# A fifth buffer for the high parts and a fifth for the low parts of the streamed weights in an encoder trunk

## The chip, the cores and the metric

The kernel runs on one core of a Trainium2 chip. The metric is the device time of one execution in microseconds. Before the change the median of three runs is 1358.05 us (1356.56 to 1358.73).

## The reference, cut to what matters

Two layers work on 256 tokens of width 1024. Each layer is a half-step SwiGLU, a mixer of three branches (a state space branch S5, gated linear attention, grouped-query attention) with gates, and a second half-step SwiGLU. All of the large products have 256 rows on the one side and a weight matrix on the other.

```python
def swiglu_ffn(h, w_gate, w_up, w_down):
    return (jax.nn.silu(h @ w_gate) * (h @ w_up)) @ w_down

for i in range(DEPTH):                                   # DEPTH = 2
    x = x + 0.5 * swiglu_ffn(rms_norm(x, ffn1_norm[i]), ...)         # 1024 -> 2816 -> 1024
    h = rms_norm(x, mix_norm[i])
    (s5_u, gla_q, gla_k, gla_v, gla_g, gla_zf, gla_zb, at_q, at_k, at_v) = split(h @ w_in[i])
    y_s5, y_gla, y_attn = s5_branch(...), gla_branch(...), attn_branch(...)
    gates = sigmoid(h @ w_merge_gate[i] + b_merge_gate[i])           # one gate for each branch
    merged = sum over the branches of gate * (y @ w_branch)
    x = x + merged @ w_out[i]
    x = x + 0.5 * swiglu_ffn(rms_norm(x, ffn2_norm[i]), ...)
return rms_norm(x, final_norm)
```

## The kernel before

**Products in three parts.** Weights and activations are float32. Each is split into a high part (hi), which is the value rounded to the type that TensorE takes, and a low part (lo), which is the rest. `mm3` (L216) makes a product of 128 x 512 from three matmuls: hi by hi (L219), lo of the weight (L220), and lo of the activation (L221).

**Streaming the weights.** `load` (L193) brings weights in pieces of two k-steps of 128 rows by 512 columns, 512 KB. For each piece it takes a buffer of the pool `wraw` (5 buffers, tile `raw`), issues its DMA on SyncE's queue (L206), takes one buffer `hi` and one `lo` of the pool `whl` (4 buffers of each), casts raw into hi on ScalarE (L209), and subtracts hi from raw into lo on VectorE (L210). So a raw buffer is free once lo is made, and a pair of hi and lo is free once the last of its matmuls has run. There are 412 such pairs. A pair with 512 columns feeds 12 matmuls: two k-steps, two tiles of 128 tokens (t = 0 and 1), three parts. `stream` (L223) goes over the blocks of 512 columns of a matrix, and for each over the chunks of four k-steps; the hidden layer's blocks have four pairs each.

**Work beside the stream.** In the first and in the middle half-steps VectorE also makes the tables of the S5 branch (`s5_tables`, L529, lines L349 to L373), a layer ahead. In the mixers it carries the three branches' elementwise work and scans. `weave` (L94) interleaves these generators with the main stream. TensorE has small matmuls and transposes of these, and the transposes of the hidden activations (L298).

**What sets the order.** The kernel is written as a program of tiles; a scheduler then lays the instructions of each engine in one order, from a timeline of its own, in which a buffer that comes free earlier makes an instruction ready earlier. On the chip each engine follows its order. A buffer pool rotates, so that with four buffers the pair of piece n waits for the last matmul of piece n-4.

**Places named below.** L209 cast to hi; L210 subtraction to lo; L219 to L221 the three matmuls; L263 and L265 the norm's transposes and their scaling; L298 the hidden layer's transposes; L355 also the table `wa` of the mixer's gates, cast at L655; L980 and L1016 transposes of the gated linear attention.

Of the kernel before, what the change touches and what calls it, by code (L numbers as in the profile page):

```python
# [31 lines left out]
HD = 128  # L32
GH = 4
WPRIO = 0
WBUFS = (5, 4)
RA = 5
RG = 4
WSTEP = 2
# [87 lines left out]
class Enc:  # L126
    def __init__(self, tc, ctx, ins, out):
# [3 lines left out]
        self.const = pool("const", 1)  # L131
        self.wraw = pool("wraw", WBUFS[0])
        self.whl = pool("whl", WBUFS[1])
        self.hp = pool("hp", 1)
# [1044 lines left out]
```

## Time and profile before

| what | value |
|---|---|
| median of three runs | 1358.05 us |
| the profiled execution | 1357.79 us |
| its span, first to last instruction | 1356.0 us |
| TensorE busy in the span | 1310.3 us, 97% |
| VectorE busy | 1013.2 us, 75% |
| ScalarE busy | 703.5 us, 52% |
| granted TensorE clock, mean | 0.995 |

The profile's page gives busy time for each engine. Matmuls overlap in it: one of 512 columns has a duration of about 0.39 us, and the next starts 0.23 us after it, so time is counted from start to start. The view of waits gives, for the idle time of an engine, which instruction ended it. The view of stages gives busy time in windows of the span. The timeline lists instructions one after another, with the idle time before one in brackets.

### The profile page before, as it was taken

How to read it: one execution, taken by the hardware profiler on the slowest of the kernel's cores; microseconds unless marked ns; L12 is line 12 of the kernel's file. 1: busy time of each engine (PE TensorE's matmuls, PEld its weight loads, DVE VectorE, ACT ScalarE, POOL GpSimd, SP SyncE). 2: the span in 40 equal slices, each digit the busy share in tenths (PEclk: the TensorE clock that was granted, in tenths of full speed). 3: DMA queues.
4: the chain of work that ended last, by engine and by line, in shares of the span. 5: the costliest groups of instructions: out<-in, count | busy, mean ns of one | idle time of the engine just before them, and what ended most of it. 6: DMA issues, size and time to landing. Idle time of an engine off the chain costs nothing.

```text
span 1356.0 us, 19228 instructions
## 1 busy us (share of the span) xinstructions
PE 1310.3 (97%) x6792; PEld 1049.8 (77%) x6792; DVE 1013.2 (75%) x1794; ACT 703.5 (52%) x1106; POOL 76.9 (6%) x108
## 2 busy tenths in 40 slices
PE   7999999999999989999999999999999999999997
PEld 5877778877786778777877777888877867888886
DVE  6899985779995779997465765457899967655553
ACT  5545445547585445444354544355475854555542
POOL 1010220000100000210000000000001000000000
PEclk9999999999999989999999999999999999999999
DMA  7767666666452366666665655566665524555562
GB/s 230 189 214 232 219 226 189 202 223 218 163 182 78 117 161 208 196 208 215 195 196 180 196 164 189 187 177 217 226 210 156 174 68 148 191 177 181 183 209 77
DMA packets 201200, 249.87 MB, mean 184 GB/s; under 512 B 40856, under 2 KB 134600, under 8 KB 201104
## 3 DMA queue, kind: packets, MB, share of 16 engines
q1 hardware_dynamic: 200496, 247.59, 58.6%
q8 instruction: 53, 0.87, 0.3%
q10 hardware_dynamic: 608, 1.06, 0.2%
q14 instruction: 43, 0.35, 0.1%
HBM read 234.44 MB, written 13.11 MB: 183 GB/s over the span
## 4 chain that ended last, share of the span: by engine, by line
PE 58%; issue 18%; DVE 17%; DMA 4%; ACT 3%; POOL 1%; SPq 0%; POOLq 0%; ACTq 0%; DVEq 0%
PE mm L220 17%; PE mm L219 16%; PE mm L221 16%; DVE lo L210 5%; DVE t L349 2%; DMA raw<-in_ffn_w_gate 1%; DVE run L838 1%; DMA e<-scr 1%; PE as L1072 1%; PE ao L1094 1%; DVE run L837 1%; PE st L298 1%; ACT hi L209 1%; DMA raw<-in_ffn_w_up 1%; PE pt L263 1%
## 5 line engine op out<-in xcount | busy, mean ns | idle before, releaser
L210 DVE TENSOR_TENSOR lo<-raw,hi 128x1024 fp32r<-128x1024 f32 x412 | 499.0, 1218 | 178.8 <-ACT hi L209 174.1
L209 ACT CAST hi<-raw 128x1024 fp32r<-128x1024 f32 x412 | 427.8, 1043 | 309.0 <-PE mm L221 282.4
L220 PE MATMUL mm<-lo,hTh 128*128 128x512 f32 (+1 forms) x1120 | 444.0, 397 | 7.6 <-DVE lo L210 7.4
L219 PE MATMUL mm<-hi,hTh 128*128 128x512 f32 (+1 forms) x1120 | 436.4, 396 | 2.0 <-ACT hTh L267 2.0
L221 PE MATMUL mm<-hi,hTl 128*128 128x512 f32 (+1 forms) x1120 | 435.1, 392 | 0.0
L220 PEld LDWEIGHTS mm<-lo,hTh 128*128 128x128 f32 x1120 | 211.4, 189 | 53.0 <-DVE lo L210 11.9
L219 PEld LDWEIGHTS mm<-hi,hTh 128*128 128x128 f32 x1120 | 211.1, 189 | 44.4 <-ACT hTh L267 2.9
L221 PEld LDWEIGHTS mm<-hi,hTl 128*128 128x128 f32 x1120 | 210.7, 188 | 40.1 <-DVE hTl L268 0.2
L220 PE MATMUL mm<-lo,sThffn 128*128 128x512 f32 x352 | 138.3, 393 | 2.8 <-DVE lo L210 2.8
L221 PE MATMUL mm<-hi,sTlffn 128*128 128x512 f32 x352 | 137.4, 391 | 0.0
L219 PE MATMUL mm<-hi,sThffn 128*128 128x512 f32 x352 | 135.9, 393 | 0.0
L300 ACT CAST sThffn<-st 128x256 fp32r<-128x256 f32 x88 | 32.7, 372 | 129.9 <-PE st L298 129.5
L220 PEld LDWEIGHTS mm<-lo,sThffn 128*128 128x128 f32 x352 | 66.1, 188 | 17.7 <-DVE lo L210 3.7
L221 PEld LDWEIGHTS mm<-hi,sTlffn 128*128 128x128 f32 x352 | 66.1, 188 | 13.9
L219 PEld LDWEIGHTS mm<-hi,sThffn 128*128 128x128 f32 x352 | 66.0, 188 | 13.6
L301 DVE TENSOR_TENSOR sTlffn<-st,sThffn 128x256 fp32r<-128x256 f32 x88 | 37.1, 423 | 48.8 <-ACT sThffn L300 48.3
L294 ACT ACTIVATE t<-mm,rstd 128x256 f32<-128x256 f32 x88 | 41.5, 475 | 43.5 <-PE mm L221 41.1
L295 DVE SCALAR_TENSOR_TENSOR t<-mm,rstd,t 128x256 f32<-128x256 f32 x88 | 41.8, 482 | 13.6 <-ACT t L294 13.4
L298 PE MATMUL st<-ident,t 128*128 128x128 f32 x176 | 33.4, 272 | 0.5 <-DVE t L295 0.5
L298 PEld LDWEIGHTS st<-ident,t 128*128 128x128 f32 x176 | 24.3, 140 | 12.1 <-DVE t L295 0.9
L349 DVE TENSOR_TENSOR t<-e,S 128x512 f32<-128x512 f32 x32 | 20.2, 683 | 17.3 <-DMA e<-scr 17.2
L627 POOL COPY kx<-ks 128x128 f32<-128x128 f32 x32 | 18.9, 630 | 218.7 <-DVE ks L610 218.7
(357 smaller groups left out, 1440.0 us busy)
## 6 DMA issues: line engine op xcount, KB each, us to landing
raw<-in_ffn_w_gate SPq DMA_DIRECT2D x176, 256.0 KB, 3.8
raw<-in_ffn_w_up SPq DMA_DIRECT2D x176, 256.0 KB, 4.3
raw<-in_ffn_w_down SPq DMA_DIRECT2D x88, 512.0 KB, 4.6
raw<-in_w_in SPq DMA_DIRECT2D x48, 512.0 KB, 3.9
raw<-in_w_merge_gate SPq DMA_DIRECT2D x48, 512.0 KB, 4.6
raw<-in_w_out SPq DMA_DIRECT2D x16, 512.0 KB, 4.4
scr<-e SPq DMA_DIRECT2D x6, 768.0 KB, 5.5
e<-scr SPq DMA_DIRECT2D x6, 768.0 KB, 5.7
```

The source lines that it names most:

```text
L209: nc.scalar.copy(hi[:, :e - s, :width], raw[:, :e - s, :width])
L210: nc.vector.tensor_tensor(lo[:, :e - s, :width], raw[:, :e - s, :width], hi[:, :e - s, :width].bitcast(F32), op=ALU.subtract)
L219: nc.tensor.matmul(ps, act[0], w[0], start=first, stop=False)
L220: nc.tensor.matmul(ps, act[0], w[1], start=False, stop=False)
L221: nc.tensor.matmul(ps, act[1], w[0], start=False, stop=last)
L294: nc.scalar.activation(sg, ps[:, :256], AF.Silu, scale=rstd[:, t:t + 1])
L295: nc.vector.scalar_tensor_tensor(s, ps[:, 256:], rstd[:, t:t + 1], sg, op0=ALU.mult, op1=ALU.mult)
L298: nc.tensor.transpose(pt[:, j], s[:, j * P:(j + 1) * P], self.ident)
L300: nc.scalar.copy(h, pt)
L301: nc.vector.tensor_tensor(sl[:, 2 * b:2 * b + 2, t * P:(t + 1) * P], pt, h.bitcast(F32), op=ALU.subtract)
L349: self.nc.vector.tensor_tensor(out, a, b, op=ALU.mult)
L627: nc.gpsimd.tensor_copy(kx[:, :, s], ks.rearrange("p g j f -> p g (j f)")[:, :, (3 - s) * 16:(3 - s) * 16 + 64])
```

## The change

The constant that holds the number of buffers of `wraw` and of `whl` goes from (5, 4) to (5, 5). The pool `whl` holds hi and lo, so there is one more tile of each: 4 KB in each partition apiece, 8 KB together. The instructions are the same; the pair of piece n now waits for the last matmul of piece n-5. The scheduler makes a new order from it.

```diff
-WBUFS = (5, 4)
+WBUFS = (5, 5)
```

TensorE, at the end of the first half-step's hidden layer. mm290 and mm291 are the results of the last block for t = 0 and t = 1; hi_285, hi_288, hi_300 and hi_303 with lo_286 to lo_304 are its four pairs; hi_313 is the first pair of the next matrix. Before:

```order
L221 MATMUL mm291_1680<-hi_288_1675,hTl4_120 128x512
L219 MATMUL mm291_1680<-hi_300_1736,hTh4_119 128x512
L220 MATMUL mm291_1680<-lo_301_1737,hTh4_119 128x512
L221 MATMUL mm291_1680<-hi_300_1736,hTl4_120 128x512
L298 MATMUL st279_1624<-ident_79,t_279_1621 128x128 x2
L219 MATMUL mm291_1680<-hi_300_1736,hTh4_119 128x512
L220 MATMUL mm291_1680<-lo_301_1737,hTh4_119 128x512
L221 MATMUL mm291_1680<-hi_300_1736,hTl4_120 128x512
L219 MATMUL mm291_1680<-hi_303_1743,hTh4_119 128x512
L220 MATMUL mm290_1679<-lo_304_1744,hTh4_119 128x512
L221 MATMUL mm290_1679<-hi_303_1743,hTl4_120 128x512
L219 MATMUL mm290_1679<-hi_303_1743,hTh4_119 128x512
```

Now, at the same place:

```order
L221 MATMUL mm290_1679<-hi_300_1736,hTl4_120 128x512
L219 MATMUL mm290_1679<-hi_303_1743,hTh4_119 128x512
L220 MATMUL mm290_1679<-lo_304_1744,hTh4_119 128x512
L221 MATMUL mm290_1679<-hi_303_1743,hTl4_120 128x512
L219 MATMUL mm290_1679<-hi_303_1743,hTh4_119 128x512
L220 MATMUL mm290_1679<-lo_304_1744,hTh4_119 128x512
L221 MATMUL mm290_1679<-hi_303_1743,hTl4_120 128x512
L298 MATMUL st276_1615<-ident_79,t_276_1612 128x128 x2
L219 MATMUL mm291_1680<-hi_285_1668,hTh4_119 128x512
L220 MATMUL mm291_1680<-lo_286_1669,hTh4_119 128x512
L221 MATMUL mm291_1680<-hi_285_1668,hTl4_120 128x512
L219 MATMUL mm291_1680<-hi_285_1668,hTh4_119 128x512
```

Before, the fourth pair (lo_304) came after t = 1 had used the first three, for both tokens' tiles together; now t = 0 uses all of the four pairs, and then t = 1 begins with the first. The last matmuls of the first three pairs stand later in the block.

VectorE, at the same place: the subtraction lo_314, for the first pair of the next matrix, among table work. Before:

```order
L364 TENSOR_TENSOR U0_1062<-ef_416,eg_417 128x512
L365 TENSOR_TENSOR U1_1063<-ef_416,eg_417 128x512
L301 TENSOR_TENSOR sTlffn10_170<-st276_1615,sThffn10_169 128x2x128
L366 TENSOR_TENSOR U2_1064<-ef_416,eg_417 128x512
L368 TENSOR_TENSOR U3_1065<-ef_416,eg_417 128x512
L364 TENSOR_TENSOR T0_1118<-bb_297_1726,lpb_414 128x512
L365 TENSOR_TENSOR T1_1119<-bb_297_1726,lpb_414 128x512
L366 TENSOR_TENSOR T2_1120<-bb_297_1726,lpb_414 128x512
L368 TENSOR_TENSOR T3_1121<-bb_297_1726,lpb_414 128x512
L210 TENSOR_TENSOR lo_314_1798<-raw_312_1795,hi_313_1797 128x1024
L210 TENSOR_TENSOR lo_317_1804<-raw_315_1801,hi_316_1803 128x1024
```

Now:

```order
L210 TENSOR_TENSOR lo_304_1744<-raw_302_1740,hi_303_1743 128x1024
L301 TENSOR_TENSOR sTlffn10_170<-st255_1507,sThffn10_169 128x2x128
L364 TENSOR_TENSOR T0_1118<-bn_170_1067,coef_413 128x8x16
L295 SCALAR_TENSOR_TENSOR t_276_1612<-mm263_1529,rstd4_117,t_275_1611 128x256
L365 TENSOR_TENSOR T1_1119<-bn_171_1086,coef_413 128x8x16
L295 SCALAR_TENSOR_TENSOR t_279_1621<-mm264_1530,rstd4_117,t_278_1620 128x256
L366 TENSOR_TENSOR T2_1120<-bn_170_1067,coef_413 128x8x16
L368 TENSOR_TENSOR T3_1121<-bn_171_1086,coef_413 128x8x16
L210 TENSOR_TENSOR lo_314_1798<-raw_312_1795,hi_313_1797 128x1024
L369 TENSOR_TENSOR e_175_1123<-U0_1062,U1_1063 128x512
L373 TENSOR_TENSOR e_175_1123<-U2_1064,U3_1065 128x512
```

The subtraction stood behind eight rows of 512 columns and one of 256; these rows (U from ef and eg, T from bb and lpb) are behind it now, and shorter rows are ahead of it.

VectorE, in the first mixer: lo_657 among the work of the state space branch (t, run, e) and of the gated linear attention (la). Before:

```order
L210 TENSOR_TENSOR lo_654_3516<-raw_652_3513,hi_653_3515 128x1024
L349 TENSOR_TENSOR t_550_3055<-e_545_3038,run0_2591 128x512
L349 TENSOR_TENSOR t_552_3057<-e_545_3038,run0_2591 128x512
L355 TENSOR_TENSOR la0_3078<-t_561_3085,la0_3078 128x2x256
L355 TENSOR_TENSOR la0_3078<-t_562_3089,la0_3078 128x2x256
L355 TENSOR_TENSOR la0_3078<-t_565_3099,la0_3078 128x2x256
L355 TENSOR_TENSOR la0_3078<-t_566_3103,la0_3078 128x2x256
L210 TENSOR_TENSOR lo_657_3522<-raw_655_3519,hi_656_3521 128x1024
L352 TENSOR_TENSOR t_553_3058<-t_550_3055,t_552_3057 128x512
```

Now:

```order
L210 TENSOR_TENSOR lo_654_3516<-raw_652_3513,hi_653_3515 128x1024
L349 TENSOR_TENSOR t_550_3055<-e_545_3038,run0_2591 128x512
L349 TENSOR_TENSOR t_552_3057<-e_545_3038,run0_2591 128x512
L355 TENSOR_TENSOR t_551_3056<-t_550_3055,t_552_3057 128x512
L210 TENSOR_TENSOR lo_657_3522<-raw_655_3519,hi_656_3521 128x1024
L349 TENSOR_TENSOR t_550_3055<-e_545_3038,run0_2591 128x512
L349 TENSOR_TENSOR t_552_3057<-e_545_3038,run0_2591 128x512
L355 TENSOR_TENSOR la0_3078<-t_561_3085,la0_3078 128x2x256
L355 TENSOR_TENSOR la0_3078<-t_562_3089,la0_3078 128x2x256
L355 TENSOR_TENSOR la0_3078<-t_565_3099,la0_3078 128x2x256
L355 TENSOR_TENSOR la0_3078<-t_566_3103,la0_3078 128x2x256
L210 TENSOR_TENSOR lo_675_3632<-raw_673_3629,hi_674_3631 128x1024
```

The subtraction lo_657 has moved ahead of two multiplications of the scan's results and of the four rows of la.

## Rows read from the trace of the kernel before

**Rows 1.** Page, head: span; busy us (share of the span) xinstructions.
```profile
span 1356.0 us, 19228 instructions
PE 1310.3 (97%) x6792; PEld 1049.8 (77%) x6792; DVE 1013.2 (75%) x1794; ACT 703.5 (52%) x1106; POOL 76.9 (6%) x108
```
**Rows 2.** Waits, whole span: engine line <- releaser: us in total, times, longest.
```profile
ACT hi L209 <- PE mm L221: 282.4, 244, 5.2
...
PE mm L220 <- DVE lo L210: 10.2, 11, 2.0
```
**Rows 3.** Waits of TensorE in windows 130:260, 260:390, 520:650, 910:1040, 1040:1170.
```profile
PE mm L220 <- DVE lo L210: 2.8, 2, 2.0
...
PE mm L220 <- DVE lo L210: 2.9, 3, 1.7
...
PE mm L220 <- DVE lo L210: 2.8, 4, 1.2
...
PE mm L220 <- DVE lo L210: 1.0, 1, 1.0
...
PE mm L220 <- DVE lo L210: 0.7, 1, 0.7
```
**Rows 4.** Stages: window, busy us (x) of PE, PEld, DVE, ACT, POOL, PEclk, DMA, GB/s.
```profile
100.00:150.00 50.00, 47.96 (x313) 38.33 (x312) 50.00 (x105) 25.69 (x40) 6.86 (x9) 1.00 0.68 220
...
350.00:400.00 50.00, 48.27 (x296) 39.92 (x294) 49.79 (x89) 34.50 (x66) 5.93 (x3) 1.00 0.56 175
...
450.00:500.00 50.00, 44.03 (x195) 34.86 (x195) 36.56 (x78) 20.80 (x30) 1.65 (x2) 0.93 0.60 170
...
1200.00:1250.00 50.00, 50.00 (x229) 40.98 (x229) 29.06 (x36) 26.02 (x37) 0.00 (x0) 1.00 0.57 177
```
**Rows 5.** Timeline of TensorE at a wait: start, duration, instruction [idle before <-releaser].
```profile
151.80 0.39 PE L219 MATMUL mm<-hi,sThffn 128*128 128x512 f32 x1
152.96 0.50 PE L220 MATMUL mm<-lo,sThffn 128*128 128x512 f32 x1 [0.77 <-DVE lo L210]
```
**Rows 6.** Timelines of ScalarE, then VectorE, from 144.41 to 149.
```profile
144.41 1.05 ACT L209 CAST hi<-raw 128x1024 fp32r<-128x1024 f32 x1 [0.27 <-PE mm L221]
...
147.28 0.68 DVE L368 TENSOR_TENSOR T<-bb,lpb 128x512 f32<-128x512 f32 x1
147.88 2.35 DVE L210 TENSOR_TENSOR lo<-raw,hi 128x1024 fp32r<-128x1024 f32 x2
```
**Rows 7.** Timeline of TensorE: two transposes; an undisturbed run, both ends.
```profile
1200.53 0.38 PE L298 MATMUL st<-ident,t 128*128 128x128 f32 x2
1200.66 0.49 PE L220 MATMUL mm<-lo,hTh 128*128 128x512 f32 x1
1200.99 0.39 PE L221 MATMUL mm<-hi,hTl 128*128 128x512 f32 x1
...
1203.07 0.39 PE L221 MATMUL mm<-hi,hTl 128*128 128x512 f32 x1
...
1210.55 0.40 PE L221 MATMUL mm<-hi,hTl 128*128 128x512 f32 x1
```
**Rows 8.** Timelines from 487 to 492: ScalarE, VectorE, TensorE.
```profile
487.59 1.04 ACT L655 CAST wa<-wraw 96x1024 fp32r<-96x1024 f32 x1 [3.11 <-DMA raw<-in_ffn_w_gate]
...
488.67 1.21 DVE L355 TENSOR_TENSOR wa<-wraw,wa 32x1024 fp32r<-32x1024 f32 x1 [2.33 <-ACT wa L655]
...
491.25 1.11 PE L263 MATMUL pt<-ident,x 128*128 128x128 f32 x4 [4.27 <-DVE t L265]
```
**Rows 9.** Waits in 260:390, then 1040:1170; then timeline of VectorE.
```profile
PE goT L1016 <- DVE t L1013: 0.3, 1, 0.3
...
PE keT L980 <- ACT aqT L1060: 1.1, 1, 1.1
...
317.46 1.22 DVE L210 TENSOR_TENSOR lo<-raw,hi 128x1024 fp32r<-128x1024 f32 x1
318.59 1.29 DVE L349 TENSOR_TENSOR t<-e,run 128x512 f32<-128x512 f32 x2
```

## The prediction, made before the changed kernel ran

> **What bounds the kernel now.** I read the page's head first, then the waits of the whole span, then the waits and the stages window by window, and last the timelines at the waits. TensorE is busy for 1310.3 of 1356.0 us [rows 1]. That share alone does not say how near the end is, since matmuls overlap. The timeline does: one matmul of 512 columns starts 0.23 us after the one before, wherever nothing is late [rows 5, 7], and the stage from 1200 to 1250 runs like that with no idle time at all [rows 4]. So TensorE is the bound, and a change of buffers can win only what TensorE waits.
>
> The largest wait in the list, 282.4 us in which ScalarE's cast to hi waits for a matmul [rows 2], is the buffer limit itself: the cast is ready, raw has landed, and no pair is free. It costs nothing by itself, since ScalarE is busy for half of the span. What costs is the wait of TensorE for lo: 10.2 us in 11 waits, the longest 2.0 us [rows 2]. They lie in four groups [rows 3]: the tables of the first half-steps (2.8 us), the first mixer (2.9), the tables of the middle half-steps (2.8), the second mixer (1.0 and 0.7). In the others TensorE never waits for lo. Two stages show why: VectorE is busy for 50.00 of 50 us from 100 to 150 and for 49.79 from 350 to 400, against 29.06 in the stage without waits [rows 4]. The wait at 149.15, the longest, shows it closest: hi was ready at 145.46, and VectorE, with no gap, did table work until 147.88 before it came to the lo for which TensorE was waiting [rows 6].
>
> So in four stretches VectorE falls behind, eats the lead that the finished pairs give, and then TensorE waits, by less than 3 us in each. The question is how much lead one more pair gives there.
>
> **The change, part by part.**
>
> *What a wait costs.* At 152.96 a matmul starts 1.16 us after the one before, where 0.23 would do [rows 5]: 0.93 lost, and the row shows 0.77 idle. So each wait costs 0.16 more than its idle time, since the modelled end of a matmul covers it. The 11 waits cost 10.2 + 11 x 0.16 = 12.0 us. That is the most that can be won from them.
>
> *What one pair gives.* A pair feeds 12 matmuls, 12 x 0.227 = 2.7 us of TensorE's work. The 0.227 is the mean of the 33 steps from 1203.07 to 1210.55, an undisturbed run [rows 7]. If all of it became lead, once in each stretch that ends behind, the stretches would lose 3.1, 3.4, 3.4 and 2.0 us (idle time and 0.16 a wait) less up to 2.7 each: 0.4, 0.7, 0.7 and 0.0 are left, 1.8 together, and 10.2 is won. But the new order spends part of the lead. Before, the fourth pair of a hidden block was used at the block's end for both tiles at once; now t = 0 uses all four pairs before t = 1 begins, so that the first pairs are held longer. I counted, in both orders, the matmuls between the last use of a pair and the first lo of the piece that gets its buffer, at 0.227 us each: 7.2 us in the mean before and 10.0 now, but in the tightest tenth 5.2 before and 6.4 now. The mean grew by a whole pair, the tightest tenth by 1.2. With 1.2 in each of the four stretches the gain is 4.8 us. The bounds are 4.8 and 12.0. I take 9, nearer to the end that the mean stands for: at the very places of the waits VectorE's order helps too, since the eight table rows that stood ahead of lo_314, and the four rows of la that stood ahead of lo_657, now stand behind it.
>
> *What moves on TensorE.* Two transposes in the stream cost 0.13 us themselves, and the matmul behind them takes 0.33 instead of 0.23 to the next [rows 7]: 0.10 for each time that the stream of weight matmuls is broken. The order before has 253 such breaks and the new one 233. 20 x 0.10 = 2 us, bounds 0 and 2. I take 2.
>
> *What moves on VectorE.* The sum of its work is the same. One lo stands further ahead all along, so work of the branches stands later by a lo, 1.13 us from start to start [rows 9]. TensorE waits for branch work in a few places today: goT 0.3 and keT 1.1 in one mixer [rows 9], and such waits can grow. If each of some six places that wait at all grows by a third of a lo, 6 x 0.4 is 2.4 us; I take 2. The bounds are 0 and 6.8 (six times 1.13).
>
> *DMA.* A raw buffer comes free when its lo is made, so the loads run up to one piece further ahead. The bytes are the same and DMA is at 0.57 of its time where TensorE is full [rows 4]; this costs nothing, and if the cover were gone it would show as casts that wait for raw.
>
> *What stays.* At 491.25, ahead of the third half-step, TensorE stands for 4.27 us. The scaling of the norm stands behind the last update of x, that behind the subtraction for the table wa, that behind its cast, which waited 3.11 us for a load [rows 8]. [...] In the new order this chain is the same, with the same loads ahead of that of wa and one weight load more. [...]
>
> *The sum.* -9 for the waits, -2 for the breaks, +2 for branch work: -9. The profiled execution took 1357.79 us, its span 1356.0 us, 0.26 us under the median of the three runs. 1358.05 - 9 = 1349.
>
> **The rivals.**
>
> *The waits move on (no change).* VectorE is full in the stretches, and its work is not reduced. If a fuller lead only lets the scheduler put more table work ahead of the next lo, TensorE waits there instead. For it: in the new order 3.9 us of table rows stand between lo_314 and lo_317, where the two followed each other. Against it: the second lo is wanted later by a piece. Of the gain of 11 some 1 to 2 would be left: 1356 to 1357.
>
> *Branch work comes late (slower).* In each mixer four heads of the gated linear attention pass through VectorE, TensorE and back, with the transposes keT (L980) and goT (L1016), 16 places in both mixers. Where a lo put ahead delays the rows of a head by 1.13 us [rows 9] and nothing covers it, TensorE, which keeps its order, waits: 16 x 1.13 = 18 us, less 12 won, makes 1364. It decides from about 11 of 16 places: then the cost passes the 12.0. For it: lo_657 stands ahead of the four rows of la now, and every head starts from la. Against it: those places wait little today [rows 9], so most have room; and TensorE would need its stream of weights to be behind them in the order everywhere. The trace bears out the order that this needs: VectorE came to lo_314 only after all rows ahead of it, though hi was ready 2.4 us earlier [rows 6]. [...]
>
> [...]
>
> **How the numbers follow.** About 0.2%, 2.7 us, is what a measurement of this kernel can tell from no change: faster is under 1355.3, slower is over 1360.8. The forecast, with its bounds (from 1358.05 - 12.0 - 2 to 1358.05 - 4.8 + 2, so 1344 to 1355), gets 0.66; the stand that goes, 0.06; waits that move on, 0.17; branch work that comes late, 0.11. The range leaves out the stand that goes and the slower rival, 0.17 together, and takes in the waits that move on, with a little room: 1343 to 1358.5. Faster is 0.72, within 0.2% is 0.17, slower is 0.11.
>
> **What would show it.** In the profile after: TensorE's waits for lo fall from 10.2 us to about 2, with single ones left in the four stretches; the casts wait less for matmuls than 282.4 us; TensorE's busy time stays within some 3 us of 1310.3, and its idle time falls by about 9. The stand at about 490 is there again with a clock of about 0.93 in its stage. Waits for keT and goT together stay under 6 us. The prediction is wrong if the waits for lo stay over 6 us (the lead is spent by the order), or if they go and the span does not follow (then the idle time is at branch work, or at the stand).

## The result, and the profile after

The changed kernel takes 1345.63 us (median of four runs, 1344.8 to 1346.58), the kernel before 1357.93 (1356.56 to 1358.73). The ratio is 0.9908, with a 95% interval of 0.9894 to 0.9923: 12.3 us or 0.9% faster. The forecast was 1349.0 with a range of 1343.0 to 1358.5. The profiled execution took 1344.8 us.

The head of the page after, which answers [rows 1]:

```profile
span 1343.0 us, 19230 instructions
PE 1305.5 (97%) x6792; PEld 1053.9 (78%) x6792; DVE 1009.0 (75%) x1794; ACT 698.2 (52%) x1106; POOL 87.6 (7%) x108
```

The span is 13.0 us shorter. TensorE's idle time, span less busy, falls from 45.7 us to 37.5, by 8.2; its busy time falls by 4.8, with the same 6792 matmuls. So more than a third of the gain is not in any wait.

Waits of the whole span, after (engine, line, releaser: us in total, times, longest), which answers [rows 2]:

```profile
ACT hi L209 <- PE mm L221: 300.6, 251, 5.8
...
ACT hi L209 <- DMA raw<-in_ffn_w_up: 14.3, 13, 3.5
...
PE mm L220 <- DVE lo L210: 4.0, 2, 2.1
```

TensorE's waits for lo fell from 10.2 us in 11 places to 4.0 in two. The casts wait longer for matmuls than before, 300.6 against 282.4.

Where the time went is read best by stage. A stage begins here with the first weight matmul of 512 columns behind the norm's transposes. In some kernels four of the sixteen transposes of a norm stand behind that matmul, so that the length of a stage is good to about 0.8 us. Stages before, in the order of the program (two half-steps with a mixer between them, for each of two layers); window, busy us of PE, PEld, DVE, ACT, POOL, then PEclk, DMA, GB/s:

```profile
10.68:217.74 207.06, 202.42 (x1093) 162.20 (x1093) 184.71 (x441) 102.13 (x146) 29.15 (x40) 1.00 0.70 215
217.74:492.02 274.28, 261.99 (x1457) 208.46 (x1457) 219.70 (x346) 158.95 (x284) 10.07 (x11) 1.00 0.56 174
492.02:693.49 201.47, 196.97 (x925) 157.89 (x924) 161.03 (x383) 95.69 (x131) 16.27 (x25) 0.99 0.64 195
693.49:893.83 200.34, 199.61 (x1023) 158.84 (x1022) 124.18 (x166) 94.37 (x135) 9.29 (x15) 1.00 0.58 183
893.83:1161.42 267.59, 260.66 (x1459) 208.39 (x1458) 216.34 (x328) 157.74 (x283) 9.10 (x8) 1.00 0.56 175
1161.42:1356.00 194.58, 186.20 (x839) 152.37 (x837) 105.47 (x127) 91.68 (x128) 1.39 (x2) 0.98 0.52 165
```

The same stages after:

```profile
10.95:213.08 202.13, 201.62 (x1097) 162.74 (x1097) 183.44 (x442) 102.51 (x148) 31.21 (x40) 1.00 0.72 222
213.08:487.37 274.29, 263.03 (x1455) 210.14 (x1454) 219.83 (x346) 157.72 (x284) 12.90 (x10) 0.99 0.56 174
487.37:682.82 195.45, 194.84 (x926) 158.51 (x924) 159.54 (x383) 95.25 (x131) 20.95 (x25) 0.99 0.65 200
682.82:877.55 194.73, 194.22 (x1023) 158.26 (x1022) 123.85 (x166) 93.73 (x135) 9.11 (x15) 1.00 0.60 188
877.55:1148.66 271.11, 263.30 (x1459) 210.12 (x1458) 217.31 (x328) 156.98 (x283) 10.38 (x8) 0.99 0.55 173
1148.66:1343.00 194.34, 186.00 (x839) 152.53 (x837) 103.21 (x126) 89.06 (x127) 1.39 (x2) 0.99 0.52 163
```

The differences are -4.9, 0.0, -6.0, -5.6, +3.5 and -0.2 us, and +0.3 ahead of the first stage: -13.0, the whole of it. The two half-steps with waits for lo won 4.9 and 6.0, most of it idle time (4.64 us to 0.51, and 4.50 to 0.61). Of these 8.0 us of idle time 5.6 were waits for lo. Another 1.3 in the first stage were a wait for a load, ahead of the transposes cT (L560) at 73.69; it is gone too. The fourth stage won 5.6 although TensorE was idle there for only 0.73 us before; its busy time fell by 5.4. The mixers, the second and the fifth stage, won nothing, and the second of them lost. (Before, four transposes stand inside the first mixer; in the changed kernel none do, so with the same work in it that mixer lost some 0.8 us too.)

**The fourth stage.** There the S5 branch makes tables for the next mixer. For each of four blocks of a layer's tables TensorE runs 48 small matmuls into `kp`, 16 of 128x32 (L597) and 32 of 64x96 (L603). Three of the four blocks are made in this stage, one in the third. Timeline of TensorE in the stage, before (start, duration, instruction, count):

```profile
782.03 0.39 PE L219 MATMUL mm<-hi,hTh 128*128 128x512 f32 x1
782.35 0.35 PE L603 MATMUL kp<-cc,bb 64*32 64x96 f32 x2
782.63 0.50 PE L220 MATMUL mm<-lo,hTh 128*128 128x512 f32 x1
782.96 0.39 PE L221 MATMUL mm<-hi,hTl 128*128 128x512 f32 x1
```

And after:

```profile
788.69 0.39 PE L221 MATMUL mm<-hi,hTl 128*128 128x512 f32 x1
789.01 0.33 PE L597 MATMUL kp<-cq,bb 128*32 128x32 f32 x16
789.27 0.56 PE L603 MATMUL kp<-cc,bb 64*32 64x96 f32 x32
789.76 0.50 PE L219 MATMUL mm<-hi,hTh 128*128 128x512 f32 x1
790.10 0.39 PE L220 MATMUL mm<-lo,hTh 128*128 128x512 f32 x1
```

Before, two small matmuls between two large ones made 0.93 us from 782.03 to 782.96, where two undisturbed steps take 0.45: 0.48 lost. After, all 48 of a block stand in one place and make 1.41 us from 788.69 to 790.10: 0.96 lost. So the price is that of the place, about 0.46, and 0.01 for each small matmul in it. In the stage's timeline before they stand in 19 places, after in 6. Thirteen places fewer at 0.46 are 6.0 us; 5.6 were won. Added up over the whole stage, the steps with such matmuls in them and the steps right behind lose 10.5 us before and 4.5 after, against 0.227 a step. The scheduler's new order did this; no wait is in it.

**The mixers.** Waits of TensorE in the windows 260:390 and 1040:1170 of after, which answer [rows 9], with the wait for lo of 910:1040 between them:

```profile
PE goT L1016 <- ACT aqT L1060: 1.5, 1, 1.5
...
PE mm L220 <- DVE lo L210: 2.1, 1, 2.1
...
PE kv L995 <- ACT t L1080: 0.9, 1, 0.9
```

Each mixer has one wait for lo now (1.93 us and 2.1), and one of 1.5 us for goT. Counted in weight matmuls from the start of the mixer, the wait for lo stands at the 535th in the first mixer and at the 536th in the second. TensorE, before, in the first mixer, at the 391st and at the 535th:

```profile
323.74 0.50 PE L220 MATMUL mm<-lo,hTh 128*128 128x512 f32 x1 [1.67 <-DVE lo L210]
...
367.09 0.50 PE L220 MATMUL mm<-lo,hTh 128*128 128x512 f32 x1 [0.74 <-DVE lo L210]
```

So the place waited before too, 0.74 us, and 0.73 at the 536th matmul of the second mixer. The earlier waits (1.67 and 0.47 us in the first mixer, 1.04 in the second) are gone; the one that is left has grown. Timeline of VectorE ahead of it in the first mixer, after (several instructions of one kind are one row):

```profile
349.88 1.22 DVE L210 TENSOR_TENSOR lo<-raw,hi 128x1024 fp32r<-128x1024 f32 x1
351.01 1.21 DVE L837 TENSOR_TENSOR_SCAN run<-e,t 64x511 f32<-64x511 f32 x1
...
356.97 1.29 DVE L349 TENSOR_TENSOR t<-e,run 128x512 f32<-128x512 f32 x2
358.17 1.22 DVE L210 TENSOR_TENSOR lo<-raw,hi 128x1024 fp32r<-128x1024 f32 x1
```

VectorE works through 7.16 us of scans and other side rows, from 351.01 to 358.17, between two subtractions. Before, subtractions at 358.51 and 362.43 stood among the same kinds of rows, and the longest stretch between two from there on was 2.79 us. TensorE at the end of it, after:

```profile
357.19 0.33 PE L855 MATMUL yp<-mt,U 64*64 64x64 f32 x4
359.45 0.75 PE L220 MATMUL mm<-lo,hTh 128*128 128x512 f32 x1 [1.93 <-DVE lo L210]
...
360.42 0.63 PE L219 MATMUL mm<-hi,hTh 128*128 128x512 f32 x1
360.85 0.63 PE L220 MATMUL mm<-lo,hTh 128*128 128x512 f32 x1
```

Behind the wait the matmuls start 0.43 us apart, not 0.23. Three windows of 3.5 us, ahead of, in and behind this stretch:

```profile
356.00:359.50 3.50, 1.57 (x11) 0.96 (x9) 3.50 (x7) 3.49 (x7) 0.57 (x1) 1.00 0.00 0
359.50:363.00 3.50, 3.50 (x11) 2.82 (x12) 3.50 (x7) 0.82 (x2) 0.00 (x0) 0.51 0.51 158
363.00:366.50 3.50, 3.50 (x17) 2.86 (x17) 3.50 (x6) 2.37 (x5) 1.44 (x1) 1.00 0.70 219
```

The 1.57 us of TensorE's work in the first window are what the wait of 1.93 leaves of it: until the wait TensorE ran large matmuls, and four small ones last. Behind the wait the granted clock was 0.51 from 359.5 to 363.0, and 1.00 again in the window after that. By an estimate from these rows, 0.49 of the work of 3.5 us is lost at 0.51 of the clock, 1.7 us; the second mixer has such a fall too, 0.52 from 1025.0 to 1028.5, about 1 us behind its wait. So the wait of 1.93 us cost about 3.6 there, by this estimate.

**The stand ahead of the third half-step** is there again, in TensorE's timeline and in the stage from 450 to 500, which answer [rows 8] and [rows 4]:

```profile
486.61 1.12 PE L263 MATMUL pt<-ident,x 128*128 128x128 f32 x4 [4.19 <-DVE t L265]
...
450.00:500.00 50.00, 44.14 (x195) 34.98 (x194) 34.63 (x80) 20.57 (x30) 1.65 (x2) 0.93 0.59 156
```

### The profile page after: what moved, and what is told of

Same layout as the page of the kernel before. It is cut to its first block, busy times and chain, and to the rows that moved or that the text cites. A ratio compares the mean times of both kernels' runs of the same rounds, so it can differ in the third digit from the quotient of the medians.

```text
span 1343.0 us, 19230 instructions
## 1 busy us (share of the span) xinstructions
PE 1305.5 (97%) x6792; PEld 1053.9 (78%) x6792; DVE 1009.0 (75%) x1794; ACT 698.2 (52%) x1106; POOL 87.6 (7%) x108
## 4 chain that ended last, share of the span: by engine, by line
PE 67%; issue 16%; DVE 10%; ACT 3%; DMA 2%; SPq 0%; POOL 0%; POOLq 0%; ACTq 0%; DVEq 0%
PE mm L219 20%; PE mm L220 19%; PE mm L221 19%; DVE lo L210 3%; PE st L298 1%; DVE t L349 1%; ACT hi L209 1%; DMA raw<-in_ffn_w_up 1%; PE as L1072 1%; DVE run L838 1%; PE ao L1094 1%; PE S L820 1%; DVE run L837 1%; PE yp L858 1%; PE apt L1087 1%
## 5 line engine op out<-in xcount | busy, mean ns | idle before, releaser
L209 ACT CAST hi<-raw 128x1024 fp32r<-128x1024 f32 x412 | 427.7, 1043 | 330.9 <-PE mm L221 300.6
L617 POOL TENSOR_TENSOR e<-r,tcst 128x512 f32<-128x512 f32 x8 | 25.4, 3180 | 152.0 <-DVE r L349 82.4
L298 PEld LDWEIGHTS st<-ident,t 128*128 128x128 f32 x176 | 23.8, 140 | 10.2
```

The lines of the kernel that those rows point to most:

```text
L209: nc.scalar.copy(hi[:, :e - s, :width], raw[:, :e - s, :width])
L298: nc.tensor.transpose(pt[:, j], s[:, j * P:(j + 1) * P], self.ident)
L617: nc.gpsimd.tensor_tensor(ld["e"][:, SCR_R - SCR_E:].rearrange("p (g c) -> p g c", g=GQ), self.r4[:, gs].unsqueeze(2).to_broadcast((P, GQ, ...
```

## The experiments

My theory after the result had three parts: the fifth pair gives lead in the half-steps with tables, the new order groups the small matmuls, and the mixers give something back. The rivals: lo alone or hi alone does it; the loads do it; grouping is a by-product that costs nothing by itself. "Stage" below is the length of a stage, found as above.

**A fifth lo alone, a fifth hi alone, more raw buffers.** Three kernels with one size changed each:

```diff
-                lo = self.whl.tile([P, SUB, 512], F32R, name=self.nm("lo"), tag="lo")
+                lo = self.whl.tile([P, SUB, 512], F32R, name=self.nm("lo"), tag="lo", bufs=5)
```

> Five buffers for lo, four for hi. The order of every engine is that of the kernel before, row for row; only the rotation of the lo buffers differs. Theory 'lead' (TensorE stops waiting because finished pairs run further ahead): a lo needs its hi, and the fifth hi is missing, so nothing runs ahead: the time of before, 1358 us within 0.2%, waits of TensorE for lo about 10 us. Theory 'order' (the gain is the scheduler's new order and has little to do with waits): the same time too, since the order is the old one. A faster time by 3 us or more would say that the lo buffers alone were what bound.

Measured: 1358.2 us, ratio 1.0001 (0.999 to 1.0011). The order is that of before.

```diff
-                hi = self.whl.tile([P, SUB, 512], F32R, name=self.nm("hi"), tag="hi")
+                hi = self.whl.tile([P, SUB, 512], F32R, name=self.nm("hi"), tag="hi", bufs=5)
```

> Five buffers for hi, four for lo: the casts can run a piece further ahead, the subtractions on VectorE cannot. The order changes: the stream of weight matmuls is broken 245 times where before has 253 and the full change 233, and in the first half-step of the second layer 31 times as in the full change (43 before). Theory 'lead': TensorE's waits for lo stay near 10 us, and only the second layer's first half-step gains, about 4 to 5 us: 1353 to 1354. Theory 'order': most of the gain of the full change, 1346 to 1350. Theory 'the cast was what bound': the waits for lo go to 4 us or under, with 1346 to 1349.

Measured: 1349.38 us, ratio 0.9944 (0.9929 to 0.9959).

```diff
-WBUFS = (5, 4)
+WBUFS = (7, 4)
```

> The same 8 KB a partition given to the raw buffers, 7 instead of 5, with four pairs. TensorE, VectorE, ScalarE and GpSimd have the order of before row for row; only SyncE's queue changes, and loads run up to two pieces further ahead. Theory 'lead': buffers help only as finished pairs; 1358 us within 0.2%, waits for lo about 10 us. Rival 'loads were late' (the fifth pair helped because it freed raw buffers sooner): 1350 or less. The stand of TensorE at 490, behind the small loads, could change by a few us either way, since the weight loads ahead of them are two more.

Measured: 1357.46 us, ratio 0.9998 (0.9984 to 1.0012). TensorE's waits for lo are 9.8 us in 10 places in the kernels with a fifth lo and with seven raw buffers. With a fifth hi:

```profile
PE mm L220 <- DVE lo L210: 7.4, 8, 1.3
```

A lo without its hi, or raw without a pair, gives nothing: the cast is what waits, and it needs a hi. So late loads, the rival, don't explain the gain. A hi alone gives some 8 us, though 7.4 of the 10.2 us of waits stay. The order explains part of that: in the fourth stage, which has no waits for lo, it takes 195.7 us against 200.3.

**The fifth pair in the half-steps alone.** In half-steps every fifth piece takes a pair of its own; in mixers four pairs turn over, as before.

```diff
+                self.piece += 1
+                five = not self.mixing and self.piece % 5 == 4
+                hi = self.whl.tile([P, SUB, 512], F32R, name=self.nm("hi"), tag="hi5" if five else "hi", bufs=1 if five else 4)
+                lo = self.whl.tile([P, SUB, 512], F32R, name=self.nm("lo"), tag="lo5" if five else "lo", bufs=1 if five else 4)
```

> The fifth pair is used in the half-steps alone; in the mixers the pairs rotate over four as before. Theory 'lead', stage by stage: the half-steps shorten as in the full change (4.9 + 6.0 + 5.6 + 0.2 us = 16.7), the mixers keep the time of before (274.3 and 267.6 us): 1341 to 1342, below the full change, whose second mixer is 3.5 us longer. Theory 'scatter of the scheduler' (each new order shifts some microseconds at random): no such sum, anywhere from 1342 to 1356.

Measured: 1345.08 us, ratio 0.9904 (0.9889 to 0.9918). The time was missed by 3 to 4 us: the half-steps with waits keep their gain (202.3 and 194.2 us), the mixers take 272.4 and 269.6, but the fourth stage takes 197.4 instead of 194.7. That is not the small matmuls, which stand in 6 places there too. TensorE is idle for 2.3 us of that stage, against 0.5 in the changed kernel: at its start the norm's transposes wait 1.11 us (at 682.23) and a matmul 0.69 (at 685.24) for VectorE's part of the norm.

**The grouping alone, with four pairs.** The small matmuls of a block get the scheduler's high priority, so that nothing is put between them while they are ready:

```diff
+            with self.tc.high_priority():
             for i in range(2):
                 for a in range(4):
...
                     nc.tensor.matmul(kp[0][a * 32:(a + 1) * 32, :, 0], lt, cpar[:, 2 * i, :, a], start=i == 0, stop=i == 1)
```

> No buffer more than before (five raw, four pairs). The 48 small matmuls of a table block (kp) get a high priority, so that they stand together in TensorE's order: in the second layer's first half-step the stream is broken 31 times (43 before), 4 times by kp (17 before), as in the full change. Theory 'grouping': the 5.6 us that the full change won in that half-step, where no wait for lo existed, come from this, so that half-step takes 195 to 197 us (200.3 before) with four pairs; the waits for lo in the first half-steps stay about 5 to 6 us; total 1352 to 1354. Theory 'lead alone': without a fifth pair nothing is won, 1358 us within 0.2%.

Measured: 1348.17 us, ratio 0.9925 (0.9906 to 0.9944), more gain than expected. The fourth stage in it, and its waits for lo in the whole span:

```profile
689.34:883.81 194.47, 193.43 (x1023) 158.01 (x1022) 124.46 (x166) 94.88 (x135) 9.79 (x15) 1.00 0.60 189
```

```profile
PE mm L220 <- DVE lo L210: 7.6, 10, 1.7
```

194.5 us, with the small matmuls in 5 places, where the changed kernel has 6: the order alone, without any buffer, gives the whole 5.6 us of this stage. The rest was not expected: the third stage (198.8) and the first mixer (270.8) are 2.7 and 3.5 us shorter, the first stage and the second mixer 1.2 longer each. The third stage has its small matmuls in 3 places instead of 6. In the first mixer 1.1 us are waits for lo (1.8 against 2.9), 0.5 the stand ahead of the third half-step, and some 0.8 are transposes that stand ahead of the stage here; the kernel with a fifth lo, which has the order of before, waits 1.8 us for lo in that mixer too. So little of the 3.5 can be put down to the grouping.

**The grouping together with the change.** Both edits, (5, 5) and high priority.

```diff
-WBUFS = (5, 4)
+WBUFS = (5, 5)
...
+            with self.tc.high_priority():
```

> The fifth pair together with the grouping of the kp matmuls: 222 breaks of the stream against 233. Theory 'lead and grouping are two things': the first half-steps as in the full change, a further 0.35 us for each of the 11 breaks less, 1342 to 1344. Theory 'the scheduler's order scatters': 1340 to 1350 with no relation to the breaks.

Measured: 1343.83 us, ratio 0.9895 (0.9877 to 0.9914), as expected. That is 1.8 us under the changed kernel by the medians, and the intervals of the two ratios overlap; without the fifth pair the same grouping won 9.8 us. The gains don't add up, since the change already holds most of the grouping.

**One more pair, paid with raw buffers; one pair fewer.**

```diff
-WBUFS = (5, 4)
+WBUFS = (3, 6)
```

> The same space as the full change, split as three raw buffers and six pairs. The distance from the last use of a pair to the first lo of the piece that takes its buffers grows from 10.0 us to 13.4 in the mean (7.2 before), 9.8 in the tightest tenth; 208 breaks of the stream. Theory 'lead': the waits for lo in the mixers (4.0 us in the full change) go too, 1338 to 1342. Rival 'loads come late with three raw buffers' (a load takes about 4.3 us to land, cast and subtraction 2.2 more, of the 8.2 us in which three pieces are used): casts wait for loads, TensorE waits for lo at new places, 1348 or more.

Measured: 1383.24 us, ratio 1.0197 (1.0158 to 1.0236).

```diff
-WBUFS = (5, 4)
+WBUFS = (5, 3)
```

> One pair less than before (five raw, three pairs). The distance from last use to first lo falls to 5.8 us in the mean (7.2 before), 4.3 in the tightest tenth; 266 breaks. Theory 'lead': VectorE needs about 2.3 us of that for hi and lo themselves, so the stretches in which it is full cost far more: waits for lo 25 to 50 us, 1375 to 1400. Theory 'order and grouping alone': 13 more breaks at 0.35 us, 1362 to 1365.

Measured: 1376.41 us, ratio 1.0135 (1.011 to 1.0159). Waits with (3, 6), then with (5, 3):

```profile
ACT hi L209 <- DMA raw<-in_ffn_w_up: 128.6, 80, 6.4
```

```profile
PE mm L220 <- DVE lo L210: 17.6, 13, 4.3
```

With three raw buffers the casts wait for loads, and six pairs can't be filled: the first half-step takes 220.7 us. With three pairs the waits for lo grow from 10.2 to 17.6 us, and the same half-step takes 220.2. In that half-step one pair fewer costs 13 us, one more wins 5. Of the 13 us 5.4 are waits for lo (8.2 against 2.8); the small matmuls also stand in 15 places there instead of 10, and the granted clock is 0.54 from 178.5 to 182.2, behind the longest wait. So the lead is real, and the 13 us are not all lead.

**The fifth pair in the mixers alone.** The edit of the half-steps with the condition turned round.

```diff
+                five = self.mixing and self.piece % 5 == 4
```

> The fifth pair in the mixers alone, the half-steps rotate over four as before. Theory 'lead and grouping act in the half-steps': half-steps as before, the mixers as in the full change (274.3 and 271.1 us against 272.4 to 274.3 and 267.6 to 269.6 in the runs with four pairs), so 1358 to 1362, no gain. Theory 'the waits for lo cost what they show in the mixers too' (2.9 and 1.7 us before, 1.9 and 2.1 in the full change): 1357 to 1358.

Measured: 1363.12 us, ratio 1.0035 (1.0019 to 1.005): slower. Its two largest waits in the first mixer are those of the changed kernel in size (a wait of 1.1 us for a load, at uT L805, is its own):

```profile
PE mm L223 <- DVE lo L213: 1.9, 1, 1.9
PE goT L1021 <- ACT aqT L1065: 1.5, 1, 1.5
```

The mixers take 274.9 and 271.2 us in it. Over the three kernels with five pairs and five raw buffers in the mixers (changed, grouping with the change, this one) the means are 274.4 and 271.1; over six with four pairs and five or more raw buffers there (before, fifth lo, seven raw buffers, fifth pair in the half-steps, grouping alone, and the last kernel below) 272.5 and 269.0. So the fifth pair costs the mixers 1.9 and 2.1 us. This was shown by doing the part alone. Most of it goes with the clock. Leaving aside the stand at the end of the first mixer, the clock falls once in either mixer in the profiled execution of each of the three kernels, behind the wait for lo, as above (0.51 and 0.52 over 3.5 us in the changed kernel, 1.7 us each by that estimate); in none of the six does it fall there (in the kernel before it is 1.00 from 323.5 to 327.0, behind its longest wait for lo in the mixers, 1.67 us).

**Five pairs, four raw buffers.** Is the raw pool still large enough?

```diff
-WBUFS = (5, 4)
+WBUFS = (4, 5)
```

> Four raw buffers and five pairs: the full change less one raw buffer. Theory 'raw buffers are not short at five': within 0.3% of the full change, 1345 to 1349, with casts that wait a little more for loads. Rival 'loads have no room': between the full change and the kernel with three raw buffers (1383 us), 1352 to 1365, TensorE waiting for lo again in the first half-steps, behind casts that wait for loads.

Measured: 1355.42 us, ratio 0.999 (0.9978 to 1.0002).

```profile
ACT hi L209 <- DMA raw<-in_ffn_w_up: 40.5, 23, 4.2
```

The casts wait 40.5 us for one matrix's loads instead of 14.3, and the gain is nearly gone. The fifth pair needs the fifth raw buffer.

**The fifth pair in the half-steps, and the grouping.** What the experiments point to:

```diff
+                five = not self.mixing and self.piece % 5 == 4
...
+            with self.tc.high_priority():
```

> The fifth pair in the half-steps alone, and the kp matmuls grouped. If the stages are independent, their spans add: half-steps as with the fifth pair and grouping (201.7, 194.5, 194.5, 194.4 us), mixers as with four pairs (272.4 and 269.6), head 10.9: a span of 1338, a time of 1340. Theory 'a fifth pair in the mixers costs nothing': the same as fifth pair and grouping everywhere, 1343 to 1344.

Measured: 1338.37 us (1336.85 to 1341.58), ratio 0.9857 (0.9842 to 0.9872). The first mixer in it, then two waits of its whole span (the fourth stage takes 194.2 us):

```profile
212.71:484.64 271.93, 261.87 (x1461) 209.44 (x1461) 221.41 (x346) 159.85 (x285) 10.06 (x10) 1.00 0.56 177
```

```profile
PE mm L223 <- DVE lo L213: 4.2, 5, 1.0
...
ACT hi L212 <- PE mm L224: 281.8, 244, 5.7
```

It beats both kernels, 1.4% under the one before and 0.5% under the changed one. No wait for lo is over 1.0 us, and the clock of the first mixer stays at 1.00.

## Why the prediction was right, and where it was not

The time was missed by 3.4 us, inside the range. The main step was right: the waits for lo cost time and a fifth pair wins most of them. But several terms of the sum were off, with both signs, and that the time came so near is in part luck. Of the 13.0 us of the span, by the rows: the waits for lo -7.6 (6.2 of idle time and nine waits fewer at 0.16), the order of the fourth stage -5.6, the wait for a load at L560 -1.3, two falls of the clock in the mixers +3.4 (twice the estimate of 1.7); about 2 us more lie in other breaks and short waits.

**The waits for lo (-9 taken).** In the half-steps right, and at the upper bound: the 5.6 us of [rows 3] that lie in them are gone, all of them. Their own tests stand behind it, with the fifth pair there alone and with three pairs. The tightest tenth of the lead, which gave the lower bound, was too dark a view. In the mixers the step failed: of 4.6 us 4.0 are there again, at one place in each, where 0.7 had been waited before. That is the first rival, waits that move on, come true in part for these two stages: VectorE does more side work between two subtractions there, 7.16 us. With the clock behind them (0.51 and 0.52 over 3.5 us) they cost more than before; the sum had no term for that.

**The breaks (-2 taken).** Here the mechanism was seen and its size was not, and the sentence that a change of buffers can win only what TensorE waits was wrong: 5.4 of the 5.6 us of the fourth stage were busy time. The step priced each break at the 0.10 us by which the matmul behind it is late [rows 7], and took the broken-in work as paid for anyway. For two transposes that holds. For small matmuls of the tables the place itself costs 0.46 us, and the fourth stage, which has no wait to win, shows the sum: 5.6 us. The count of 253 and 233 breaks also hid that 12 of the 20 went from this one stage. The kernel with the grouping alone has 238 breaks, five more than the changed one, but 31 in that stage as the changed one has, where 43 were before, and 194.5 us: which breaks go matters, not only how many.

**Branch work (+2 taken).** Too much. keT and goT together wait 4.1 us against 3.6, under the 6 that were named, and all of it is goT now; kv, with 0.9 in each mixer, is new. But waits for other branch work (ao and as, 2.1 us before) are gone, so that the whole grew by about 0.4. The second rival, late branch work that makes the kernel slower, did not come true: four places of 16 wait, not 11.

**DMA (0 taken).** Right for the casts with five raw buffers; the wait of 1.3 us for a load at L560, which the sum didn't have, went away, and so it did with seven raw buffers. The sign named for its failure, casts that wait for raw, is there with four, and strongly with three.

**The stand at 491 (no term in the sum).** It stayed, 4.19 us against 4.27, clock 0.93 in both. The stand that goes, which had a chance of 0.06, did not come true.

**The signs.** Idle time fell by 8.2, where 9 was named. Waits for lo fell to 4.0, not 2. Busy time fell by 4.8, not within 3 of the old: this sign pointed at the mis-sized breaks. That the casts would wait less for matmuls was wrong: 300.6 us in the changed kernel, 281.8 in the faster one with the fifth pair in the half-steps, 282.4 before. The row says that pairs are what the casts wait for, and nothing on how much the span loses by it.

**What stays open.** In the half-steps the longer rotation and VectorE's new order came together in every run with a fifth pair; which of the two took the 5.6 us of waits away was not separated. Why the clock fell behind some waits of about 2 us and not behind others was not found (below). Whether another place for the scans of VectorE would take the wait at 359.45 away was not tried.

## What to carry to other kernels

One more pair took the waits away here where TensorE ran out of lead in the half-steps (5.6 us to 0), and not in the mixers (4.6 to 4.0): so take the waits stage by stage, and look for a place where the other engine's side work comes in one long stretch. Here the wait at such a place, behind 7.16 us of VectorE's side work, grew from 0.74 to 1.93 us. Where a scheduler makes the order, a buffer count is also a new order: look at a stage that has no waits, and if it changes length too, find the order's part and try it without the buffer. The small matmuls strewn into this stream of large ones cost by the place, 0.46 us, and hardly by their number: 48 in one place cost 0.96 us, twice the 0.48 of two.

## What was not expected of the hardware

A short wait cost nearly twice its length, by the estimate above 3.6 us for 1.93. In the changed kernel's first mixer the granted clock fell to 0.51 right behind that wait, at 359.45, and it fell again, to 0.52, about 1 us behind the wait of 2.1 us in the second mixer. In the kernel before, a wait of 2.04 us at 149.15 was followed by no fall:

```profile
149.15 0.50 PE L220 MATMUL mm<-lo,sThffn 128*128 128x512 f32 x1 [2.04 <-DVE lo L210]
...
149.00:152.50 3.50, 3.04 (x12) 2.17 (x12) 3.50 (x6) 0.00 (x0) 0.00 (x0) 1.00 0.56 173
```

The work ahead did not settle it here. In the kernel with seven raw buffers TensorE has the order of before; at the same place, behind the same stream of large matmuls, it waits 1.99 us, and there the clock falls to 0.50:

```profile
148.40 0.67 PE L220 MATMUL mm<-lo,sThffn 128*128 128x512 f32 x1 [1.99 <-DVE lo L210]
...
148.60:152.00 3.40, 3.40 (x9) 2.64 (x9) 3.40 (x5) 0.00 (x0) 0.00 (x0) 0.50 0.68 185
```

Over the profiled executions of all these kernels there are 16 waits for lo of 1.9 to 2.3 us; behind 10 of them the clock fell, behind 6 it did not. With four raw buffers and five pairs a wait of 1.90 us stands at the same place of either mixer, at 364.70 and at 1031.29, and only the second is followed by a fall (matmuls 0.43 us apart from 1034.29 to 1035.57; 0.23 behind the first). With three pairs one of 3.03 us, at 156.11, is followed by none (0.23 us apart). So such a wait put 1.7 us, by the estimate above, at risk in these runs, and neither its length nor the work ahead of it told whether they were lost; the cause stays open.
